# A low weight part made by a second ScalarE copy and an adding DMA, for one weight tile in eight

## The chip, the cores and the metric

The kernel runs on one core of one Trainium2 chip. The metric is the device time of one execution in microseconds. Five engines matter here: PE (TensorE, with its weight loads PEld), DVE (VectorE), ACT (ScalarE), POOL (GpSimd) and SP, whose queue issues the weight loads; 16 DMA engines move the data.

## What is computed

A decoder trunk of two layers on 256 tokens of 2048 features, all in fp32, each layer followed by an MLP with 8192 hidden units:

```
x += nsa_mixer(rmsnorm(x))        # three attention branches, one over compressed blocks
x += square(relu(rmsnorm(x) @ w_up[0])) @ w_down[0]
k, v = shared_kv(x)
x += diff_mixer(rmsnorm(x), k, v) # differential attention
x += square(relu(rmsnorm(x) @ w_up[1])) @ w_down[1]
out = rmsnorm(x)
```

Nearly all of the arithmetic is products of activations with weights. To keep fp32 accuracy each operand is cut into a high part, rounded to the type fp32r, and a low part, which is what the rounding left over; a product is then made of three matmuls (high by high, high by low, low by high).

## The kernel before

All weights pass through one stream, `plan`, of 368 units of 512 rows by 512 columns. A unit is two halves of 256 rows; a half is a tile of 128 partitions by 1024 elements (512 KB). `issue_raw` loads a half into a `raw` buffer by a DMA of SP's queue, `issue_split` makes from it the high part `wh` and the low part `wl`, and `unit_mm` or `up_unit` multiplies. `advance`, called as each unit is taken, issues loads up to four units ahead and splits up to two. Each of the tags `raw`, `wh` and `wl` has four buffers, so two units: a load waits until the split of the half two units earlier is done with `raw`, and a split waits until PE is done with the `wh` and `wl` of the half two units earlier.

The split is two instructions, line 146 on ACT and line 147 on DVE:

```
nc.scalar.activation(h, src, AF.Copy)
nc.vector.tensor_tensor(l, src, h.bitcast(F32), ALU.subtract)
```

The order of the work on PE and SP is that of the program; the other engines' queues are ordered by the scheduler, with the splits at high priority, and every queue is worked off in order. Attention heads, transposes and the norms are pieces that are put between the steps of the stream by a count of PE's time.

Stages of the stream by unit: 0 to 7 (first projections), 8 to 39 (projections, each followed by a unit of the compression product, which has only eight matmuls), 40 to 55 (queries, with heads between), 56 to 71 (output projection), 72 to 199 (first MLP: in each of four groups 16 up units, then 16 down units), 200 to 239 (keys, values, queries and output of the second layer), 240 to 367 (second MLP). In up units, `up_unit`, the weights are the stationary operand, and both halves are used until near the unit's end: the first half until three quarters of it. In the others the weights are the moving operand, and the first half is done in the middle of the unit.

Of the kernel before, what the change touches and what calls it, by code (L numbers as in the profile page):

```python
# [11 lines left out]
AF = mybir.ActivationFunctionType  # L12
ALU = mybir.AluOpType
AX = mybir.AxisListType

P = 128
# [4 lines left out]
EPS = 1e-6  # L21
NEG = -3.0e38
FLOOR = -1.0e38
# NSA heads: waits before the scores, the transposes and the values; head to head; first head
WAIT_A = (2.0, 12.5, 4.0, 1.5, 7.0)
# differential heads: the same, and before the normed output's transposes
WAIT_B = (1.0, 8.5, 5.0, 5.5, 9.0, 7.0)
LAMBDA_INIT = 0.8 - 0.6 * math.exp(-0.3 * 1)

# [2 lines left out]
def kernel(  # L32
# [22 lines left out]
    nc = tc.nc  # L55
# [14 lines left out]
    def T(shape, tag, dt=F32):  # L70
        return sb.tile(shape, dt, tag=tag, name=name(tag), bufs=BUFS[tag])
# [3 lines left out]
    def PT(tag):  # L75
        return pp.tile([P, 512], F32, tag=tag, name=name(tag), bufs=PB[tag])

# [1 line left out]
    # The weight products run as a steady stream; the pieces that wait on other  # L79
    # engines are generators, resumed between the stream's steps once the time  # L80
    # that they asked for has gone by on the tensor engine's own count.
    clock = [0.0]
    tasks = []
    seq = [0]
# [22 lines left out]
    def tick():  # L107
        if tasks and tasks[0][0] <= clock[0]:
            step()
# [21 lines left out]
    def mm(o, l, r, start, stop, shared=False):  # L131
        nc.tensor.matmul(o, lhsT=l, rhs=r, start=start, stop=stop, skip_group_check=shared)  # L132
        clock[0] += max(o.shape[-1], 256) / 2400.0

    def transpose(o, i, idn):
        nc.tensor.transpose(o, i, idn)  # L136
        clock[0] += 0.11
# [6 lines left out]
    def split(h, l, src, scale=None):  # L144
        if scale is None:
            nc.scalar.activation(h, src, AF.Copy)  # L146
            nc.vector.tensor_tensor(l, src, h.bitcast(F32), ALU.subtract)  # L147
        else:
            nc.scalar.activation(h, src, AF.Copy, scale=scale)
            nc.vector.scalar_tensor_tensor(l, src, scale, h.bitcast(F32), ALU.mult, ALU.subtract)  # L150

    ctx.enter_context(tc.manual_schedule(engines={mybir.EngineType.PE, mybir.EngineType.SP}))

# [1 line left out]
    cst = cp.tile([P, 640], F32, name="cst")  # L155
    ident = cst[:, 0:128]
    cmask = cst[:, 128:384]
# [20 lines left out]
    gates = cp.tile([P, 2, 48], F32, name="gates")  # L178
# [14 lines left out]
    def g_kv(k):  # L193
        return gcol2[:, 32 + k:33 + k]

# [1 line left out]
    plan = []  # L197

    def add_units(w, rows, c0):
# [12 lines left out]
        add_units(win, range(4), c * 512)  # L212

    def out_order():
        # (column chunk, head group): the later a group's heads come out, the later its part
        return ([(0, 0), (1, 0), (0, 1), (1, 1), (2, 0), (2, 1), (3, 0), (3, 1)] + [(2, 2), (3, 2), (0, 2), (1, 2)]
                + [(c, 3) for c in range(4)])

# [4 lines left out]
        add_units(nsa_w_out[0], [g], c * 512)  # L223

    def down_order(last):
        # (column chunk, quarter of the group's rows); at the very end the last quarters of two
        # chunks stay on chip and are used for one token tile after the other
        if not last:
            return [(c, u) for c in range(4) for u in range(4)]
        return ([(c, u) for c in range(2) for u in range(4)] + [(c, u) for c in (2, 3) for u in range(3)]  # L230
                + [(2, 3), (3, 3)])
# [17 lines left out]
    raws = {}  # L249
    units = {}  # L250
# [14 lines left out]
    def issue_split():  # L265
        i = pos["split"]
        if i >= len(plan):
            return
        pos["split"] += 1
        us = []  # L270
        for r in raws.pop(i):
            h = T([P, 2, 512], "wh", F32R)
            l = T([P, 2, 512], "wl", F32R)
            split(h, l, r)
            us.append((h, l))
        units[i] = us

# [20 lines left out]
                    start and kk == 0, stop and kk == 3)  # L298
                tick()

# [1 line left out]
    def new_stats():  # L302
        return T([P, 2, 4], "ss"), T([P, 2], "rs")

# [28 lines left out]
                          tp[:, kk * 256:(kk + 1) * 256], gf(k))  # L333

    def new_xt():
        # two tiles of eight feature blocks: [feature, block, part, token]
        return [T([P, 8, 2, S], "big", F32R) for _ in range(2)]

    def rope(dst, src, n, rot, ct, stb):
# [17 lines left out]
        return o  # L357

    def transpose_k(src, th, tl):
        # th, tl: [dk, kv head, token block, token]  # L360
        for pr in range(2):
            if pr:
                yield 0.8
            tp = PT("tp")
            for hh in range(2):
                for t in range(2):
                    h = pr * 2 + hh
                    transpose(tp[:, hh * 256 + t * P:hh * 256 + (t + 1) * P],
                              src[:, t, h * P:(h + 1) * P], ident)
            hs = slice(2 * pr, 2 * pr + 2)  # L370
            split(th[:, hs], tl[:, hs], tp.rearrange("p (h t q) -> p h t q", h=2, t=2))
# [5 lines left out]
    def new_kv(*shape):  # L377
        return T([P, *shape], "kv", F32R)


# [1 line left out]
    with tc.high_priority():  # L382
        for c in range(4):
            if c == 0:
# [16 lines left out]
        nc.vector.tensor_scalar(gsub, gcol2[:, 48:49], 1.0 - LAMBDA_INIT, None, ALU.mult)  # L401
        yield 0.0

    # =========================== layer 0: NSA ===========================
    ss, rs = new_stats()
    xt = new_xt()
    xts = [spawn(xt_chunk(c, [(lambda k: g_attn(0, k), xt)]), 5.5 * c - 2.0) for c in range(4)]
# [58 lines left out]
        X.append(T([P, 32, 120], "big", F32R))  # L466
        tX.append(spawn(make_X(tok, X[j], j)))

    # gates: the stationary operand holds both parts of the weights side by side
    gwp = [T([P, 8, 96], tag, F32R) for tag in ("wh", "wl")]  # L470
    for i in range(2):
        split(gwp[i][:, :, 0:48], gwp[i][:, :, 48:96], gw[:, 8 * i:8 * i + 8, :])
# [89 lines left out]
    half = cp.tile([P, 1], F32, name="half")  # L562
# [139 lines left out]
        return done  # L702

    def up_unit(us, ps, xt, k0):
        # weights stationary: the product comes out with the hidden units on partitions, the
        # part with the high half of the activations and the one with the low half side by side
        for pair in range(2):
            for kk in range(4):
                wh, wl = us[kk // 2]
                k = k0 + kk  # L710
                both = xt[k // 8][:, k % 8].rearrange("p s q -> p (s q)")
                for b in (2 * pair, 2 * pair + 1):
                    bs = slice(b * P, (b + 1) * P)
                    mm(ps[b], wh[:, kk % 2, bs], both, k == 0, False)
                    mm(ps[b][:, 0:S], wl[:, kk % 2, bs], both[:, 0:S], False, k == 15)
                tick()
# [75 lines left out]
    mlp(0, mxt, rs2, hook0, done)  # L792
    finish_stats(ssd, rsd)

    # =========================== layer 1: differential attention ===========================
    lamt = T([P, 256], "sbt")
    nc.gpsimd.dma_start(lamt, diff_lambda.rearrange("b f d -> b (f d)").to_broadcast([P, 256]))
    lv = lamt.rearrange("p (a b d) -> p a b d", a=2, b=2)
# [10 lines left out]
    ps = proj(kxt, before=xts)  # L809
    t_ = evac_tok(ps, rsd)  # L810
    rope(t_, t_, 8, 16, cosB, sinB)
    # keys of the two components side by side, each with zeros on the other's rows:
    # [.., kv head, (first tile: c0, c1; second tile: c0, c1), key]
    dkh, dkl, dv = new_kv(4, 4, P), new_kv(4, 4, P), new_kv(2, 4, 2, P)
    for d in (dkh, dkl):
        for cc in range(2):
            r = slice(64 - cc * 64, 128 - cc * 64)
# [18 lines left out]
    ready = [spawn(diff_keys(), 6.0)]  # L836
    ps = proj(kxt)
    for t in range(2):
        # [key, key tile, kv head, part, value column]
        split(dv[:, t, :, 0, :], dv[:, t, :, 1, :], ps[t].rearrange("p (g d) -> p g d", g=4), rsd[:, t:t + 1])  # L840

    oth, otl = T([P, 16, 256], "big", F32R), T([P, 16, 256], "big", F32R)
# [2 lines left out]
    def diff_head(hd, qr):  # L845
        g, i = hd // 4, hd % 4
# [44 lines left out]
        yield WAIT_B[2]  # L891
        yield from s_o.take()
        o = PT("tp")
        # columns: (first tile: main, low part of the values; second tile: the same)
        for t, blocks in ((0, ((0, 0),)), (1, ((1, 0), (2, 1)))):
            for n, (s_, kt) in enumerate(blocks):
                a = slice(s_ * P, (s_ + 1) * P)
# [68 lines left out]


def _consts():
    """Identity, causal masks and rotary tables: they depend on the shapes alone."""
    import numpy as np  # L970

    c = np.zeros((128, 640), np.float32)
    p = np.arange(128)
    c[:, 0:128] = np.eye(128, dtype=np.float32)
    c[:, 256:384] = np.where(p[None, :] <= p[:, None], 0.0, NEG)
    n = np.arange(32)
    for t in range(2):
        ok = (n[None, :] < 15) & (16 * n[None, :] + 31 <= (t * 128 + p)[:, None])
        c[:, 384 + 32 * t:416 + 32 * t] = np.where(ok, 0.0, NEG)

    def tables(head_dim, o):
        rot = head_dim // 4
        h = rot // 2
        e = (np.arange(0, rot, 2, dtype=np.float32) / np.float32(rot)).astype(np.float32)
        inv = (np.float32(1.0) / np.power(np.float32(500000.0), e)).astype(np.float32)
        ang = np.arange(S, dtype=np.float32)[:, None] * inv[None, :]
        cos, sin = np.cos(ang).astype(np.float32), np.sin(ang).astype(np.float32)
        for t in range(2):
            r = slice(t * 128, (t + 1) * 128)
            c[:, o + t * rot:o + t * rot + h] = cos[r]  # L990
            c[:, o + t * rot + h:o + (t + 1) * rot] = cos[r]
            b = o + 2 * rot + t * rot
            c[:, b:b + h] = -sin[r]
            c[:, b + h:b + rot] = sin[r]

    tables(128, 448)
    tables(64, 576)
    return c
# [24 lines left out]
```

## Time and profile before

| | |
|---|---|
| median of 3 runs | 2161.58 us (2161.39 to 2163.61) |
| profiled execution, span from the first to the last instruction | 2159.3 us |
| PE busy | 2135.1 us, 99% of the span |
| DVE busy | 1333.7 us, 62% |
| ACT busy | 1082.7 us, 50% |
| POOL busy | 81.4 us, 4% |
| read from HBM | 390.5 MB |

The span is that of one profiled execution, and the durations of its rows come from that one; the median is 2.3 us above it. Matmuls are pipelined: the record of one overlaps the next, so the step from one start to the next tells its pace.

### The profile page before, as it was taken

The numbers are of one execution on the slowest core, as the hardware profiler recorded it, in microseconds if no ns is written. First come the engines' busy times: TensorE is split into PE (matmuls) and PEld (weight loads), VectorE is DVE, ScalarE is ACT, GpSimd is POOL, SyncE is SP. The second block draws the span as 40 slices with busy tenths as digits, with TensorE's granted clock in tenths as the row PEclk, the third lists the DMA queues.
The fourth block names the chain that finished last, engine by engine and source line by source line (L and its number), as shares of the span: only waits on it lengthen the run. The fifth ranks groups of instructions, "written<-read, shape, count | busy, mean of one in ns | idle before, by whom it ended". The sixth has DMA issues, their size and how long they took to land.

```text
span 2159.3 us, 28803 instructions
## 1 busy us (share of the span) xinstructions
PE 2135.1 (99%) x10780; PEld 1794.7 (83%) x10780; DVE 1333.7 (62%) x2156; ACT 1082.7 (50%) x1737; POOL 81.4 (4%) x121
## 2 busy tenths in 40 slices
PE   8999999999999999999999999999999999999998
PEld 6877888888888888888888877888888888888886
DVE  5665777666546656555666578866656655655654
ACT  6665666454434434434555466664434434544443
POOL 0111100000000000000000111000000000000000
PEclk9999999999999999999999999999999999999999
DMA  7787432455566566666655543356566556566654
GB/s 244 238 266 242 124 100 90 145 171 184 196 194 189 193 194 186 195 195 188 188 191 185 185 146 127 127 186 188 193 194 186 195 194 187 187 199 190 192 193 142
DMA packets 204828, 394.45 MB, mean 183 GB/s; under 512 B 14176, under 2 KB 14368, under 8 KB 204560
## 3 DMA queue, kind: packets, MB, share of 16 engines
q1 hardware_dynamic: 203936, 390.51, 57.2%
q0 software_dynamic: 560, 2.02, 0.3%
q8 instruction: 84, 1.38, 0.3%
q14 instruction: 56, 0.46, 0.1%
q10 hardware_dynamic: 192, 0.08, 0.0%
HBM read 390.47 MB, written 2.10 MB: 182 GB/s over the span
## 4 chain that ended last, share of the span: by engine, by line
PE 94%; DVE 2%; ACT 1%; DMA 1%; issue 1%; POOL 0%; SPq 0%; DVEq 0%; POOLq 0%; ACTq 0%
PE acc L132 59%; PE tp L132 33%; PE tp L136 2%; DVE wl L147 1%; DMA raw<-in_nsa_w_in_dram 1%; ACT wh L146 1%; DMA raw<-in_nsa_cmp_w_dram 0%; ACT sa L874 0%; ACT sbt L874 0%; POOL sq L910 0%; DVE psl L147 0%; DVE big L150 0%; DVE sbt L881 0%; DVE pwl L906 0%; DVE pwl L912 0%
## 5 line engine op out<-in xcount | busy, mean ns | idle before, releaser
L147 DVE TENSOR_TENSOR wl<-raw,wh 128x1024 fp32r<-128x1024 f32 x736 | 902.4, 1228 | 711.9 <-ACT wh L146 705.4
L146 ACT ACTIVATE wh<-raw 128x1024 fp32r<-128x1024 f32 x736 | 777.8, 1058 | 825.4 <-PE acc L132 489.3
L132 PE MATMUL acc<-wh,big 128*128 128x512 f32 (+1 forms) x1600 | 548.0, 403 | 1.3 <-ACT wh L146 1.3
L132 PE MATMUL acc<-wh,kv 128*128 128x512 f32 x1280 | 397.2, 390 | 0.0
L132 PE MATMUL tp<-big,wh 128*128 128x512 f32 (+1 forms) x1040 | 359.5, 392 | 0.0
L132 PE MATMUL acc<-big,wh 128*128 128x512 f32 x1024 | 357.9, 394 | 0.0
L132 PEld LDWEIGHTS acc<-wh,big 128*128 128x128 f32 (+1 forms) x1600 | 300.9, 188 | 67.4 <-ACT wh L146 1.7
L132 PE MATMUL acc<-wl,big 128*128 128x512 f32 (+1 forms) x832 | 329.1, 396 | 0.5 <-DVE wl L147 0.5
L132 PE MATMUL tp<-big,wl 128*128 128x256 f32 (+1 forms) x1040 | 288.9, 280 | 0.0
L132 PE MATMUL acc<-big,wl 128*128 128x256 f32 x1024 | 286.8, 280 | 0.0
L132 PEld LDWEIGHTS acc<-wh,kv 128*128 128x128 f32 x1280 | 240.3, 188 | 50.1
L132 PE MATMUL acc<-wl,kv 128*128 128x512 f32 x640 | 249.0, 389 | 0.0
L132 PE MATMUL tp<-wh,kv 128*128 128x512 f32 x768 | 237.4, 389 | 0.0
L132 PEld LDWEIGHTS tp<-big,wh 128*128 128x128 f32 (+1 forms) x1040 | 194.3, 187 | 44.0
L132 PEld LDWEIGHTS acc<-big,wh 128*128 128x128 f32 x1024 | 192.3, 188 | 43.6
L132 PEld LDWEIGHTS tp<-big,wl 128*128 128x128 f32 (+1 forms) x1040 | 194.9, 188 | 0.0
L132 PEld LDWEIGHTS acc<-big,wl 128*128 128x128 f32 x1024 | 192.9, 188 | 0.2
L132 PEld LDWEIGHTS acc<-wl,big 128*128 128x128 f32 (+1 forms) x832 | 156.7, 188 | 31.3 <-DVE wl L147 1.0
L132 PEld LDWEIGHTS tp<-wh,kv 128*128 128x128 f32 x768 | 144.2, 188 | 29.9
L132 PE MATMUL tp<-wl,kv 128*128 128x512 f32 x384 | 149.4, 389 | 0.0
L132 PEld LDWEIGHTS acc<-wl,kv 128*128 128x128 f32 x640 | 120.2, 188 | 24.4
L146 ACT ACTIVATE kv<-q 128x256 fp32r<-128x256 f32 x128 | 50.0, 412 | 73.4 <-DVE q L735 73.4
(183 smaller groups left out, 1416.7 us busy)
## 6 DMA issues: line engine op xcount, KB each, us to landing
raw<-in_mlp_w_up_dram SPq DMA_DIRECT2D x256, 512.0 KB, 3.9
raw<-in_mlp_w_down_dram SPq DMA_DIRECT2D x256, 512.0 KB, 4.3
raw<-in_nsa_w_in_dram SPq DMA_DIRECT2D x80, 512.0 KB, 4.4
raw<-in_nsa_cmp_w_dram SPq DMA_DIRECT2D x32, 512.0 KB, 4.8
raw<-in_nsa_w_out_dram SPq DMA_DIRECT2D x32, 512.0 KB, 3.7
raw<-in_diff_w_q_dram SPq DMA_DIRECT2D x32, 512.0 KB, 3.7
raw<-in_diff_w_out_dram SPq DMA_DIRECT2D x32, 512.0 KB, 3.7
raw<-in_kv_w_shared_dram SPq DMA_DIRECT2D x16, 512.0 KB, 3.5
```

The costliest lines, as they stand in the source:

```text
L132: nc.tensor.matmul(o, lhsT=l, rhs=r, start=start, stop=stop, skip_group_check=shared)
L136: nc.tensor.transpose(o, i, idn)
L146: nc.scalar.activation(h, src, AF.Copy)
L147: nc.vector.tensor_tensor(l, src, h.bitcast(F32), ALU.subtract)
```

## The change

For the first half of every fourth unit (i % 4 = 2; 92 of 736 tiles) the low part is made in another way. ACT writes the high part `h` as before, then a second copy with the factor -1 into the buffer of the low part, which is minus the high part, and a DMA issued by POOL adds the weights to it in place. In every second of these tiles (i % 8 = 2) the DMA's source is the `raw` buffer on the chip, in the others it is the weights in HBM, read a second time. The other tiles stay as they were. The rest of the diff takes out comment lines.

```
-        for r in raws.pop(i):
+        for hf, r in enumerate(raws.pop(i)):
             h = T([P, 2, 512], "wh", F32R)
             l = T([P, 2, 512], "wl", F32R)
-            split(h, l, r)
+            if hf == 0 and i % 4 == 2:
+
+                nc.scalar.activation(h, r, AF.Copy)
+                nc.scalar.activation(l, r, AF.Copy, scale=-1.0)
+                src = r if i % 8 == 2 else plan[i][0:256].rearrange("(k p) c -> p k c", p=P)
+                nc.gpsimd.dma_start(l, src, accum_op=ALU.add)
+            else:
+                split(h, l, r)
             us.append((h, l))
         units[i] = us
```

## Rows read from the trace of the kernel before

**Rows 1.** The page's first line and the busy time of each engine.

```profile
span 2159.3 us, 28803 instructions
PE 2135.1 (99%) x10780; PEld 1794.7 (83%) x10780; DVE 1333.7 (62%) x2156; ACT 1082.7 (50%) x1737; POOL 81.4 (4%) x121
```

**Rows 2.** The chain that ended last, its shares of the span by engine.

```profile
by line: PE acc L132 59.3%; PE tp L132 32.6%; PE tp L136 2.2%; DVE wl L147 0.9%; DMA raw<-in_nsa_w_in_dram 0.8%; ACT wh L146 0.6%; issue 0.6%; DMA raw<-in_nsa_cmp_w_dram 0.2%; ACT sa L874 0.2%; ACT sbt L874 0.2%; POOL sq L910 0.2%; DVE psl 
```

**Rows 3.** Waits of PE: us in total, times, longest us.

```profile
PE tp L136 <- DMA cst<-in_consts_dram: 5.8, 1, 5.8
PE tp L136 <- DVE pwl L912: 1.9, 3, 1.2
...
PE acc L132 <- ACT wh L146: 1.3, 1, 1.3
...
PE tp L132 <- DVE qtl L147: 0.8, 2, 0.6
PE tp L132 <- DVE big L150: 0.7, 1, 0.7
PE tp L136 <- DVE pwl L906: 0.5, 1, 0.5
PE acc L132 <- DVE wl L147: 0.5, 1, 0.5
```

**Rows 4.** Timeline, compression stage, unit 22: start us, us, instruction [idle before <-releaser].

```profile
113.86 1.06 ACT L146 ACTIVATE wh<-raw 128x1024 fp32r<-128x1024 f32 x1 [1.45 <-PE acc L132]
...
118.55 0.40 PE L132 MATMUL acc<-wl,big 128*128 128x512 f32 x1
```

**Rows 5.** Timeline, first MLP, up products, unit 118.

```profile
706.88 1.05 ACT L146 ACTIVATE wh<-raw 128x1024 fp32r<-128x1024 f32 x1
...
707.96 2.50 DVE L147 TENSOR_TENSOR wl<-raw,wh 128x1024 fp32r<-128x1024 f32 x2 [0.53 <-ACT wh L146]
...
713.56 0.19 PEld L132 LDWEIGHTS tp<-big,wl 128*128 128x128 f32 x1
```

**Rows 6.** Timeline, first MLP, down products, unit 130.

```profile
771.12 1.06 ACT L146 ACTIVATE wh<-raw 128x1024 fp32r<-128x1024 f32 x1 [1.66 <-PE tp L132]
...
779.31 0.39 PE L132 MATMUL tp<-wl,kv 128*128 128x512 f32 x1
```

**Rows 7.** Timeline, values of the second layer, unit 206.

```profile
1192.49 1.06 ACT L146 ACTIVATE wh<-raw 128x1024 fp32r<-128x1024 f32 x1 [1.11 <-PE acc L132]
...
1201.79 0.39 PE L132 MATMUL acc<-wl,big 128*128 128x512 f32 x1
```

**Rows 8.** Groups of instructions: the two steps of a split.

```profile
L147 DVE TENSOR_TENSOR wl<-raw,wh 128x1024 fp32r<-128x1024 f32 x736 | 902.4, 1228 | 711.9 <-ACT wh L146 705.4
L146 ACT ACTIVATE wh<-raw 128x1024 fp32r<-128x1024 f32 x736 | 777.8, 1058 | 825.4 <-PE acc L132 489.3
```

**Rows 9.** DMA issues of POOL's queue: KB each, median us from issue to landing.

```profile
big<-in_final_norm_g_dram POOLq DMA_DIRECT2D x1, 1024.0 KB, 7.9
...
sbt<-in_diff_lambda_dram POOLq DMA_DIRECT2D x1, 128.0 KB, 3.4
```

**Rows 10.** SP's queue: packets, MB, share of 16 engines; then its up loads.

```profile
q1 hardware_dynamic: 203936, 390.51, 57.2%
...
raw<-in_mlp_w_up_dram SPq DMA_DIRECT2D x256, 512.0 KB, 3.9
```

**Rows 11.** Windows: length, busy us of each engine, PEclk, DMA share, GB/s.

```profile
68.00:195.00 127.00, 125.57 (x555) 100.15 (x554) 88.31 (x86) 78.14 (x85) 13.68 (x19) 1.00 0.85 269
...
625.00:1130.00 505.00, 505.00 (x2598) 431.63 (x2597) 294.02 (x361) 230.56 (x300) 0.00 (x0) 1.00 0.61 191
```

**Rows 12.** Waits of SP's queue: us in total, times, longest us.

```profile
SPq L261 <- DVE wl L147: 1413.6, 588, 10.2
```

**Rows 13.** The chain in order of time: one chunk of four up units.

```profile
702.62 22.19 PE tp L132 x128
```

**Rows 14.** Groups of POOL: the longest instruction of a rotary pass.

```profile
L351 POOL TENSOR_TENSOR q<-q,rb 128x256 f32<-128x256 f32 x11 | 12.0, 1090 | 0.9
```

## The prediction

> **What bounds the kernel now.** I read the page's head first: PE is busy for 2135.1 us of a span of 2159.3, DVE for 1333.7, ACT for 1082.7, POOL for 81.4 [rows 1]. The chain that ended last is PE in the weight products for nine tenths of its length, and DVE's `wl` has 1% of it [rows 2]. So the kernel is a stream of matmuls, with 24 us in which PE is idle. Then I asked what PE waited for: the longest wait is the load of constants at the start (5.8 us); a weight tile's high part cost it 1.3 us and a low part 0.5 us, once each in 736 tiles [rows 3]. Nothing that makes DVE faster can give back more than these crumbs. What counts is the reverse: by how much a low part may come later before PE stands still.
>
> **The room that each low part has.** With four `wh` and four `wl` buffers, the tile for unit i can be split only after PE has finished the tile two units earlier; ACT's idle time before `wh` is indeed put down to PE [rows 4, 6]. From that start I measured to the first PE instruction that reads the low part, for one unit of each kind that the edit touches (i with i % 4 = 2, first half). In the stage with the compression products (units 8 to 39, where short units of eight matmuls alternate with long ones): ACT starts at 113.86, the matmul is at 118.55, 4.69 us [rows 4]. In the up products: 706.88 to the weight load at 713.56, 6.68 us [rows 5]. In the down products: 771.12 to 779.31, 8.19 us [rows 6]. In the others, between which attention heads run, I show 1192.49 to 1201.79, 9.30 us [rows 7]. Now the low part is there early: in the up unit DVE begins at 707.96 and needs 1.25 us, so it ends 2.3 us after ACT's start, with 4.4 us to spare.
>
> **The change part by part.** There are 368 units, so 92 tiles are touched: 9 with the short room (8 in the compression stage and unit 2), 32 up, 32 down, 19 others.
>
> Removed: 92 subtractions at 1.23 us [rows 8], 113 us of DVE. They lie beside PE, so they are worth nothing, at most the 0.5 us that PE once waited for `wl` [rows 3].
>
> Added on ACT: 92 copies of the same shape as `wh<-raw`, 1.06 us each [rows 8], 97.5 us. ACT goes from 50% to 55% busy. The second half's copy queues behind the new one, so its low part (on DVE as before) comes up to 1.06 us later, inside a room of some 4 us; I take nothing. Without that cover it would be 92 x 1.06 = 98 us.
>
> Added on the path: the low part is now copy, copy, DMA issued by POOL, landing. The two copies and hand-overs take 2.2 us (2 x 1.06 plus an estimated 0.1), about what copy and subtraction take now. Then the whole landing time L of the adding DMA comes on top: a tile delays PE by 2.2 + L minus its room, where that is positive. PE takes its matmuls in order, so everything behind that one waits, and nothing later gives the time back.
>
> L is not in the trace, since no DMA of before adds. POOL's own DMAs bound it: 128 KB landed in 3.4 us, 1024 KB, among loads like the MLP's, in 7.9 us [rows 9]. The line through these two is 2.76 us + 5.02 ns per KB, so a plain 512 KB takes 5.3 us. An add must read two operands of 512 KB each; if each byte read counts, that is 1024 KB, 7.9 us. With the price of the SP queue's loads instead (57.2% of 2159.3 us for 745 loads of 512 KB is 1.66 us each [rows 10]) twice that on top of 2.76 us is 6.1 us, free of the loads that share the engines. Those are there: the DMA engines are 61% busy in the MLP stages and 85% in the compression stage [rows 11]. I take 7.0, midway between 6.1 and 7.9. The outer bounds are 3.4 us (the smallest transfer of POOL's queue) and 7.9 us.
>
> With L = 7.0 the chain is 9.2 us: 9 tiles x (9.2 - 4.69) = 40.6 us; 32 up x (9.2 - 6.68) = 80.6; 32 down x (9.2 - 8.19) = 32.3; the other 19 have room. The sum is 153.5 us. At 5.3 it is 25.3 + 26.2 = 51.5 us; at 7.9 it is 48.7 + 109.4 + 61.1 + 15.2 = 234 us; at 3.4 only 9 x 0.91 = 8 us.
>
> The skill has a price for L. The Trainium skill, DMA: Bandwidth & Descriptors (Anatomy of one DMA — SWDGE path), fits POOL's DMAs with 2.0 us plus bytes over 436 GB/s; for 1024 KB that is 4.4 us, and the sum would be 9 x (6.6 - 4.69) = 17 us. By that fit 128 KB would take 2.3 us, where the trace shows 3.4 [rows 9], so I hold to the rows. The Trainium skill, Collectives: The Full Stack (The bandwidth ceiling), finds an adding transfer 1.93 times as slow as a copy, because it reads two sources; by it L would be 2.76 + 1.93 x 2.57 = 7.7 us and the sum 216 us; no row here shows an add.
>
> Moved buffers: for the 46 tiles that add from `raw`, the buffer comes free when the DMA lands, not when DVE has read it. SP's queue waits for exactly that release already (1413.6 us in total [rows 12]), and it is in order, so the next loads start late too. In an up unit the load would start 9.2 us after the split, not 2.3, land 3.9 us later [rows 10], at 13.1, while its own split, two units of 5.55 us later (a chunk of four units takes 22.19 us [rows 13]), is due at 11.1 plus the stall of 2.5, so at 13.6. Just in time: nothing; if that cover is gone, the split's 4.4 us to spare comes next. The other 46 read their weights a second time, 24 MB on 390, and free `raw` a little earlier: nothing.
>
> POOL's queue: what stands behind a waiting DMA there are the rotary steps and the powers for the norms, 81.4 us in all [rows 1]; behind a rotary pass (six instructions, the longest of 1.1 us [rows 14]) the DMA can itself be late. POOL is busy for 13.7 us of the 127 of the compression stage [rows 11], so one of its nine tiles may meet such a pass: below 6.6 us, left out.
>
> **The rivals.** (a) The add costs little: L between 3.4 and 5.3, the read of the second operand hidden or the fixed part smaller, as by the fit above. Then only the compression stage and a sliver of the up products stall: 8 to 50 us, 2170 to 2212 us. For it: the SP queue lands 512 KB in 3.9 us [rows 10]. Against it: POOL's 128 KB needs 3.4.
> (b) It costs more: L above 7.9, or PE's clock falls after stalls. At L = 10 the sum is 67.6 + 176.6 + 128.3 + 55.1 = 428 us, 2589 us. The clock: all rows before are at 1.00 of 2.4 GHz [rows 11], and PE never idled over 1.3 us for a weight [rows 3], so nothing here shows what stalls of 2.5 to 4.5 us do. At the lower level, 1.2 GHz, one unit takes another 5.5 us; after the 9 longest stalls that is 50 us (2365), after all 41 above 2.5 us 226 us (2541).
> (c) The other side, not slower: the chain ends before PE comes. The place that decides is the compression stage: 2.2 + L must stay within 4.69, so L up to 2.5 us. Then the time is 2161.6 less at most the 0.5 us of [rows 3] (more only if DVE's 113 us free the few waits for its other results, 4.4 us in all with it [rows 3]). Against it: no POOL DMA of 128 KB or more lands under 3.4 us [rows 9].
>
> **How the numbers follow.** The profiled execution's span is 2159.3 us, the median of the runs 2161.58, 2.3 above it; I add to the median: 2161.6 + 153.5 = 2315 us. Chances: forecast (L 5.3 to 7.9, 2213 to 2396 us) 0.60; (a) 0.20; (b) 0.15; (c) 0.05, most of it no change. A measurement of this kernel tells about 0.2% (4.3 us) from no change. (a) and (b) are slower as well, so slower 0.95, same 0.04, faster 0.01. The range goes from the bound of L at 3.4, 2170, to L = 8.8 (56.8 + 138.2 + 89.9 + 32.3 = 317 us), 2480; it leaves out (c) and the greater part of (b).
>
> **What would show it.** Right: PE's waits in the changed profile name the low part's DMA in 70 to 90 tiles, longest in the compression stage (near 4.5 us), 2.5 us in up, 1 us in down products; issue to landing near 7 us; PE's busy time about the same and its idle time 24 + 150 us; up chunks of four units at 24.7 us for 22.19. Wrong: landings under 5 us (a), over 8 us or a granted clock under 1.00 inside the span (b), SP or ACT named as what PE waits for (then `raw` is late and the cover above was none), or no new wait (c).

## The result and the profile after

The changed kernel takes 2342.5 us (median of 4 runs, 2341.8 to 2346.6) for 2161.5 before; the ratio is 1.084, with a 95% interval from 1.0827 to 1.0854. The prediction was 2315 us, range 2170 to 2480. The profiled execution has a span of 2344.8 us for 2159.3, 185.5 us more.

The page's head after; it answers to [rows 1].

```profile
span 2344.8 us, 29065 instructions
PE 2204.6 (94%) x10780; PEld 1832.4 (78%) x10780; DVE 1219.9 (52%) x2064; ACT 1165.6 (50%) x1829; POOL 170.9 (7%) x213
```

PE has the same 10780 matmuls. Its busy time is 69.5 us longer, and its idle time went from 24.2 to 140.2 us, 116.0 more; 69.5 + 116.0 is the whole difference. So there are two losses, one in waiting and one in matmuls that themselves take longer.

What PE waited for, after (us in total, times, longest us); it answers to [rows 3].

```profile
PE tp L132 <- DMA wl<-in_mlp_w_up_dram: 52.7, 16, 4.6
PE acc L132 <- DMA wl<-in_nsa_w_in_dram: 23.5, 4, 6.3
PE acc L132 <- DMA wl<-in_mlp_w_down_dram: 18.9, 10, 2.7
PE acc L132 <- DMA wl<-raw: 12.4, 7, 2.4
PE tp L132 <- DMA wl<-in_mlp_w_down_dram: 7.5, 6, 2.6
...
PE acc L132 <- DMA wl<-in_kv_w_shared_dram: 0.6, 1, 0.6
```

These six lines sum to 115.6 of the 116.0 us: the added waiting is the adding DMA. They are also lopsided. The 46 adds from HBM cost 103 us, the 46 from `raw` 12. The DMA issues show why (KB each, median us from issue to landing; they answer to [rows 9]):

```profile
wl<-raw POOLq DMA_DIRECT2D x46, 512.0 KB, 5.0
...
wl<-in_mlp_w_up_dram POOLq DMA_DIRECT2D x16, 512.0 KB, 8.2
wl<-in_mlp_w_down_dram POOLq DMA_DIRECT2D x16, 512.0 KB, 9.2
...
wl<-in_nsa_w_in_dram POOLq DMA_DIRECT2D x7, 512.0 KB, 9.2
```

Two neighbouring up tiles in the timeline, first one that adds from `raw` (unit 114), then one that adds from HBM (unit 118); start us, us, instruction. The second is the tile of [rows 5].

```profile
755.48 1.06 ACT L276 ACTIVATE wh<-raw 128x1024 fp32r<-128x1024 f32 x1
756.45 1.04 ACT L277 ACTIVATE wl<-raw 128x1024 fp32r<-128x1024 f32 x1
757.78 0.91 POOL L279 DMA_DIRECT2D wl<-raw  x1 [27.89 <-ACT wl L277]
759.72 3.41 SPq L261 DMA_DIRECT2D raw<-in_mlp_w_up_dram  x2
762.78 0.19 PEld L132 LDWEIGHTS acc<-big,wl 128*128 128x128 f32 x1 [0.29 <-DMA wl<-raw]
...
778.32 1.06 ACT L276 ACTIVATE wh<-raw 128x1024 fp32r<-128x1024 f32 x1
779.29 1.04 ACT L277 ACTIVATE wl<-raw 128x1024 fp32r<-128x1024 f32 x1
780.35 7.75 SPq L261 DMA_DIRECT2D raw<-in_mlp_w_down_dram  x4
780.62 1.20 POOL L279 DMA_DIRECT2D wl<-in_mlp_w_up_dram  x1 [21.93 <-ACT wl L277]
788.08 0.19 PEld L132 LDWEIGHTS tp<-big,wl 128*128 128x128 f32 x1 [2.75 <-DMA wl<-in_mlp_w_up_dram]
```

Both have copy, copy, issue, and both issue 2.3 us after ACT's start. With `raw` as the source, SP's next load comes 1.9 us after the issue, and PE waits 0.3 us. With HBM as the source, ACT's second copy was the last reader of `raw`, so SP starts its loads at 780.35, 0.27 us before POOL's add, and the low part comes 7.5 us after its issue.

The other loss is the clock: the granted clock is the share of 2.4 GHz at which PE was let run. Four stretches around a down tile's wait, after (length, busy us of PE, PEld, DVE, ACT, POOL, granted clock, DMA share, GB/s):

```profile
829.00:832.00 3.00, 3.00 (x15) 2.40 (x13) 1.23 (x1) 1.06 (x1) 0.00 (x0) 1.00 1.04 213
832.00:835.00 3.00, 0.29 (x2) 0.00 (x0) 1.22 (x1) 1.06 (x1) 0.00 (x0) 1.00 1.04 345
835.00:838.00 3.00, 2.98 (x7) 2.41 (x8) 0.00 (x0) 0.00 (x0) 0.00 (x0) 0.53 0.62 229
839.00:842.00 3.00, 3.00 (x15) 2.45 (x14) 1.22 (x1) 1.06 (x1) 0.00 (x0) 1.00 0.00 0
```

PE works, stands still for 2.7 us, and comes back at a granted clock of 0.53, that is nearly all at 1.2 GHz: 7 matmuls start in 3 us, not 15. Over the span the mean granted clock is 0.974, so (1 - 0.974) x 2344.8 = 61 us of full-speed time are missing (before, at 0.999, it was 2 us), most of the 69.5 us. Not each wait has this after it: from 785.4 to 788.1 PE stands still for 2.4 us (unit 118), from 1123.6 to 1127.0 for 3.4 us, longer than the wait above, and the stretches behind them are at 1.00:

```profile
785.40:788.10 2.70, 0.28 (x3) 0.03 (x1) 2.12 (x2) 1.04 (x1) 0.00 (x0) 1.00 1.00 302
788.10:792.00 3.90, 3.90 (x22) 3.44 (x23) 0.00 (x0) 0.00 (x0) 0.00 (x0) 1.00 0.65 236
...
1123.60:1127.00 3.40, 0.00 (x0) 0.00 (x0) 1.86 (x2) 0.79 (x1) 0.00 (x0) 1.00 1.01 310
1127.10:1131.10 4.00, 4.00 (x23) 3.50 (x24) 0.00 (x0) 0.00 (x0) 0.00 (x0) 1.00 0.44 156
```

### The profile page after: what moved, and what is told of

It reads as the page before. It is cut to its first block, busy times and chain, and to the rows that moved or that the text cites. A ratio compares the mean times of both kernels' runs of the same rounds, so it can differ in the third digit from the quotient of the medians.

```text
span 2344.8 us, 29065 instructions
## 1 busy us (share of the span) xinstructions
PE 2204.6 (94%) x10780; PEld 1832.4 (78%) x10780; DVE 1219.9 (52%) x2064; ACT 1165.6 (50%) x1829; POOL 170.9 (7%) x213
## 3 DMA queue, kind: packets, MB, share of 16 engines
q0 software_dynamic: 19696, 50.26, 11.8%
## 4 chain that ended last, share of the span: by engine, by line
PE 73%; DMA 15%; ACT 3%; DVE 2%; issue 1%; POOL 0%; POOLq 0%; DVEq 0%; ACTq 0%; SPq 0%
PE acc L132 46%; PE tp L132 25%; DMA wl<-in_mlp_w_down_dram 6%; DMA wl<-in_mlp_w_up_dram 6%; ACT wl L277 2%; PE tp L136 2%; DMA wl<-raw 2%; DMA wl<-in_nsa_w_in_dram 1%; DVE wl L147 1%; ACT wh L146 0%; DMA wl<-in_kv_w_shared_dram 0%; DMA raw<-in_nsa_w_in_dram 0%; ACT sbt L881 0%; ACT sa L881 0%; ACT wh L276 0%
## 5 line engine op out<-in xcount | busy, mean ns | idle before, releaser
L147 DVE TENSOR_TENSOR wl<-raw,wh 128x1024 fp32r<-128x1024 f32 x644 | 787.5, 1226 | 959.4 <-ACT wh L146 952.5
L146 ACT ACTIVATE wh<-raw 128x1024 fp32r<-128x1024 f32 x644 | 678.8, 1057 | 854.8 <-PE acc L132 461.0
L132 PE MATMUL acc<-wh,big 128*128 128x512 f32 (+1 forms) x1600 | 556.3, 409 | 1.0 <-ACT wh L146 1.0
L132 PE MATMUL acc<-wh,kv 128*128 128x512 f32 x1280 | 403.9, 396 | 0.0
L132 PE MATMUL tp<-big,wh 128*128 128x512 f32 (+1 forms) x1040 | 383.9, 411 | 0.0
L132 PE MATMUL acc<-wl,big 128*128 128x512 f32 (+1 forms) x832 | 335.5, 403 | 34.4 <-DMA wl<-in_nsa_w_in_dram 23.5
L132 PE MATMUL tp<-big,wl 128*128 128x256 f32 (+1 forms) x1040 | 302.3, 293 | 52.7 <-DMA wl<-in_mlp_w_up_dram 52.7
L132 PEld LDWEIGHTS tp<-big,wl 128*128 128x128 f32 (+1 forms) x1040 | 206.3, 199 | 57.8 <-DMA wl<-in_mlp_w_up_dram 57.8
L132 PEld LDWEIGHTS tp<-big,wh 128*128 128x128 f32 (+1 forms) x1040 | 205.7, 198 | 49.1
L132 PEld LDWEIGHTS acc<-wl,kv 128*128 128x128 f32 x640 | 122.4, 191 | 48.3 <-DMA wl<-in_mlp_w_down_dram 23.1
L277 ACT ACTIVATE wl<-raw 128x1024 fp32r<-128x1024 f32 x92 | 96.9, 1053 | 55.2 <-PE acc L132 36.8
```

The lines of the kernel that those rows point to most:

```text
L277: nc.scalar.activation(l, r, AF.Copy, scale=-1.0)
```

## The experiments

Theory: an adding DMA is late where the chain of copy, issue and landing is longer than the room of the tile's buffer; from HBM it is later because the same choice of source lets SP's loads out beside it; the lower clock comes on top of the longer waits. Rivals: one landing time for all, whatever the source; HBM reads that are slow by themselves; ACT's added copies; the added traffic. A time without an interval is that of one run; the kernel before took 2161.3 to 2163.2 us on the chips of these runs.

**All from raw, and all from HBM.** The edit of the first:

```
-                src = r if i % 8 == 2 else plan[i][0:256].rearrange("(k p) c -> p k c", p=P)
+                src = r
```

> All 92 adds read the raw buffer on the chip, none reads HBM. Theory A (what counts is the source of the add: the profile of the changed kernel lands the adds from raw in 5.0 us and those from HBM in 8 to 9 us): landing stays near 5 us for all, PE waits about 2.3 us in each of 9 tiles of the first stages and under 0.6 us in the 32 up tiles, nothing in down; some 2190 to 2200 us, granted clock above 0.99. Rival B (one L for all of about 7 us, as the prediction had it): 2300 to 2345 us.

Measured: 2210.2 us, 49 above the kernel before; landing 4.9 us; PE waits 23.1 us, all in nine tiles; mean clock 0.993. Theory A holds for the source, though the time is 10 us over its figure.

The second takes the HBM expression in all 92 tiles.

> All 92 adds read the weights from HBM a second time. Theory A: every tile behaves as the 46 from HBM do now, so the 103 us of waits on those double to some 206 us and the work lost to the lower clock (69 us of PE busy time more than before) nearly doubles too: 2450 to 2500 us, landing 8 to 9 us. Rival B (the source does not matter): unchanged, about 2340 us.

Measured: 2462.6 us; landings 8.0 to 9.1 us; the waits for the adds sum to 204 us (twice 103 is 206); mean clock 0.964. So twice the tiles from HBM give twice the waits.

**The loads held back.** In the 46 tiles from HBM a POOL instruction of one column reads `raw` and the finished low part, so that SP's next load has to wait for the landing:

```
                 nc.gpsimd.dma_start(l, src, accum_op=ALU.add)
+                if i % 8 != 2:
+                    nc.gpsimd.tensor_tensor(hold, r[:, 0, 0:1], l[:, 0, 0:1].bitcast(F32), ALU.add)
```

> After each add from HBM a one-column POOL instruction reads both the raw buffer and the finished low part, so that the next load into this raw buffer can't start before the add has landed, as it already is with the adds from raw. Theory E (the adds from HBM land late because the loads that SP then issues get into the DMA engines first): landing from HBM falls from 8 to 9 us to some 6 us and the time to 2220 to 2270 us. Rival F (reading HBM for an add is slow by itself): landing stays at 8 us or more and the time at 2340 us or above, since the loads are later.

Measured: 2246.4 us, 96 us less, with the same bytes from the same sources. The landings and PE's waits of this run:

```profile
wl<-in_mlp_w_up_dram POOLq DMA_DIRECT2D x16, 512.0 KB, 6.3
wl<-in_mlp_w_down_dram POOLq DMA_DIRECT2D x16, 512.0 KB, 7.5
wl<-in_nsa_w_in_dram POOLq DMA_DIRECT2D x7, 512.0 KB, 6.0
```

```profile
PE tp L132 <- DMA wl<-in_mlp_w_up_dram: 23.8, 16, 1.8
PE acc L132 <- DMA wl<-raw: 13.4, 6, 2.4
PE acc L132 <- DMA wl<-in_nsa_w_in_dram: 13.2, 4, 3.9
PE acc L132 <- DMA wl<-in_mlp_w_down_dram: 3.6, 5, 1.1
```

The wait in up tiles fell from 52.7 to 23.8 us and in down tiles from 26.4 to 5.5, and the mean clock is 0.993. Theory E holds in that the loads that are let out make the add late; rival F falls as the main cause, though 6.0 to 7.5 us are not yet the 4.9 of the adds from `raw`.

**One piece for two.** The adds from HBM read 128 rows of 1024 columns (`wide` holds these slices) in place of 256 rows of 512:

```
-                src = r if i % 8 == 2 else plan[i][0:256].rearrange("(k p) c -> p k c", p=P)
+                src = r if i % 8 == 2 else wide[i].rearrange("p (k c) -> p k c", k=2)
```

> The adds from HBM read 128 rows of 1024 columns of the same matrix (4 KB in one piece for each partition) in place of 256 rows of 512 (two pieces of 2 KB), so the low parts of these 46 tiles get other numbers; bytes, sources and order stay. Theory G (the number of pieces makes the adds from HBM late: POOL's issue takes 1.2 us for them and 0.9 us for those from raw): issue 0.9 us, landing 6 to 7 us, time 2250 to 2290 us. Rival (the loads that are let through set it): landing stays at 8 us and more, time 2325 us or above.

Measured: 2280.4 us. POOL's issues of this run (ns min/median/max, first and last start) against 1.20 us for the HBM ones after:

```profile
L281 POOL DMA_DIRECT2D wl<-raw x46: 853/864/953, 23.2 to 2229.5; - x46
L281 POOL DMA_DIRECT2D wl<-in_mlp_w_up_dram x16: 853/862/866, 531.8 to 2162.1; - x16
```

Issue falls by 0.34 us, landing to 7.3 us in up and 7.5 in down tiles, the up waits from 52.7 to 37.5 us. Theory G has its time, but the landings stay above the 6 to 7 us that it named. The form of the read (larger pieces, and half as many) and SP's loads both make the add late; which share each has when both are changed was not tried.

**Copy without adding.** The `accum_op` is left out.

> The 92 DMAs copy the weights into the low part's buffer without adding, so the low part is the weight itself and the products are other numbers. Theory C (the add reads two operands, so the movement takes twice that of a copy, 3.1 for 1.6 us): landings fall by about 1.5 us, to 3.5 us from raw and 7 us from HBM, and the time to 2230 to 2260 us. Rival D (the adding costs nothing, the fixed part and what is in the engines' queues cost it all): landings and time as with the add, about 2340 us.

Measured: 2217.0 us; landings 3.5 us from `raw`, 5.1 (up) and 7.1 us (down) from HBM. The engines' time for POOL's queue is 7.1% of a span of 2215.2 us, in the run with the add 11.8% of 2344.8; less the 6.5 us that the queue already took before (0.3% of 2159.3), that is 1.64 and 2.94 us for each DMA. The add takes 1.8 times a copy. Theory C holds for the price of the add, and 125 of the 181 us go with it; the up landings fell by 3.1 us, more than its 1.5, and the time is 13 us under its figure.

**The second copy alone.** The DMA goes, and DVE makes the low part again:

```
-                nc.gpsimd.dma_start(l, src, accum_op=ALU.add)
+                nc.vector.tensor_tensor(l, r, h.bitcast(F32), ALU.subtract)
```

> The second ScalarE copy stays in the 92 tiles, but the low part is then made by VectorE as in the kernel before (its subtraction overwrites the copy); no adding DMA. If the copy lies beside PE, as the prediction has it: the time of before, 2161 to 2165 us. Rival (ACT's queue is part of the loss: each copy delays the second half's high part or an attention head): up to 92 x 1.06 = 98 us more, 2180 to 2260 us.

Measured: 2167.3 us, ratio 1.0023, interval 1.0014 to 1.0033, about 5 us. The rival's 20 to 98 us did not come, but the copies are not quite free.

**Negative copy first.** The copy with -1 and the DMA stand ahead of the high part's copy.

> The negative copy and the DMA stand ahead of the high part's copy in all 92 tiles. In the profile of the changed kernel the scheduler has that order already in the down units and most others, while in the up units the high part goes first. Theory (the chain ahead of the add counts in full): each of the 16 up tiles from HBM gets its low part 0.95 us earlier, 15 us, the 16 from raw lose their stalls of some 0.3 us, and a few stretches at the lower clock go: 2310 to 2328 us. Rival (the landing alone sets it, or the loads of SP move along): unchanged at 2340 us.

Measured: 2316.8 us, within the figure. The up waits fell from 52.7 to 40.4 us, 12.3 us where 15 were expected. The landings in up tiles stayed at 8.2 us, though SP's next loads now come after the add's issue has begun. In the down units little changed (24.1 us of waits for 26.4), since there the scheduler had put the negative copy first already, as this part of the timeline of the changed kernel shows (unit 134):

```profile
871.88 1.06 ACT L277 ACTIVATE wl<-raw 128x1024 fp32r<-128x1024 f32 x1 [1.43 <-PE tp L132]
872.84 1.04 ACT L276 ACTIVATE wh<-raw 128x1024 fp32r<-128x1024 f32 x1
...
873.23 1.20 POOL L279 DMA_DIRECT2D wl<-in_mlp_w_down_dram  x1 [20.86 <-ACT wl L277]
...
873.91 9.06 SPq L261 DMA_DIRECT2D raw<-in_mlp_w_up_dram  x4
```

Here `raw` comes free only with the high part's copy, and SP's loads go out 0.7 us after the add's issue has begun. The add lands late all the same (the median is 9.2 us in down tiles), so a load need not be issued first to delay the add.

**An own buffer.** On top of that, the low part of the 92 tiles gets its own tag, with one buffer (`wx=1`), so it need not wait for PE to leave a `wl` buffer; the rotary scratch moves to another tag to make room.

```
-            l = T([P, 2, 512], "wl", F32R)
+            l = T([P, 2, 512], "wx" if hf == 0 and i % 4 == 2 else "wl", F32R)
...
-        b = T([P, 2, n, rot], "rb")
+        b = T([P, 2, n, rot], "sbt")
```

> As the run with the negative copy first, but the low part of the 92 tiles gets a buffer tag of its own (to make room for it the rotary scratch shares another tag), so that copy and add no longer wait for PE to leave a low part's buffer and can start some 3 us earlier. Same sources, same number of bytes. Theory (the whole loss is lateness at PE, the traffic itself costs nothing): nearly all of it goes, up and down stages back at the pace of before, a few us of waits left in the compression stage: 2161 to 2185 us, granted clock at 0.99 or more. Rival (the 50 MB more of adding traffic slow the weight loads or the matmuls): 2220 us or more even so.

Measured: 2207.3 us, ratio 1.0208, interval 1.0191 to 1.0225. That is 22 us over the theory's figure. The stages separate it (columns as in the windows above):

```profile
70.00:210.00 140.00, 117.81 (x478) 92.20 (x477) 66.79 (x67) 72.78 (x81) 16.82 (x23) 0.91 0.75 229
...
660.00:1160.00 500.00, 500.00 (x2573) 427.87 (x2572) 263.05 (x331) 246.31 (x312) 22.99 (x22) 1.00 0.71 215
```

The same windows of the changed kernel:

```profile
70.00:210.00 140.00, 114.49 (x467) 89.26 (x467) 64.63 (x67) 69.42 (x78) 17.75 (x24) 0.91 0.74 225
660.00:1160.00 500.00, 472.71 (x2343) 398.10 (x2342) 234.44 (x289) 218.01 (x269) 21.26 (x21) 0.98 0.66 196
```

In the first MLP PE has no idle time at all and the full clock, although the adds still take 7.3 us in up and 8.2 us in down tiles from issue to landing and the DMA engines are 71% busy. The compression stage is nearly as bad as with the shared buffer: 22 us idle in 140 for 26, clock 0.91 in both.

**An own buffer, all from raw.**

> As the run with its own buffer, and all 92 adds read raw. The raw buffer is then held until the add has landed in every tile. Theory: landing near 5 us and started early, so no low part is late, not even in the compression stage: 2161 to 2166 us, no faster than the kernel before, since PE's matmuls are the bound and VectorE's 113 us were beside them. Rival (VectorE's work taken away is worth something): below 2157 us. Rival (held raw buffers make SP's loads late): 2175 us or more, with PE or ACT waiting for loads.

Measured: 2198.6 us, ratio 1.0166, interval 1.015 to 1.0181. The figure was missed, and so was the landing near 5 us. All of PE's waits for adds, 20.3 us in 8 tiles, are in the first stages. The landings of this run, and one of the waits in the timeline:

```profile
wx<-raw POOLq DMA_DIRECT2D x92, 512.0 KB, 6.8
```

```profile
122.63 1.06 ACT L276 ACTIVATE wx<-raw 128x1024 fp32r<-128x1024 f32 x1 [0.18 <-DMA raw<-in_nsa_w_in_dram]
122.98 1.50 SPq L261 DMA_DIRECT2D raw<-in_nsa_cmp_w_dram  x2
123.99 0.85 POOL L278 DMA_DIRECT2D wx<-raw  x1 [16.43 <-ACT wx L276]
132.75 0.19 PEld L132 LDWEIGHTS acc<-wx,big 128*128 128x128 f32 x1 [4.20 <-DMA wx<-raw]
...
132.76 0.51 PE L132 MATMUL acc<-wx,big 128*128 128x512 f32 x1 [3.77 <-DMA wx<-raw]
```

Here the copy waits for its weights, which have only just come, so an own buffer gains little; SP issues two loads, the first of them a microsecond earlier than the add, and this add from `raw` takes 8.8 us too. The same adds from `raw` landed in 4.9 us with the shared buffer and in 6.8 us with an own one, which starts them earlier: the source does not decide alone, what else is under way does too.

**The control, and an own buffer from unit 40 on.** The control is the kernel before with the rotary scratch moved.

> The kernel before, with nothing changed but the rotary scratch sharing the tag of the heads' score tiles, as the two runs with an own buffer needed it. It is the control for them: in their profiles PE also stood still in the stages with attention heads. If that came from this sharing: 2170 to 2185 us. If it came from the adds: 2161 to 2165 us.

Measured: 2162.7 us, ratio 0.9998, interval 0.9989 to 1.0008: the move costs nothing, so the move of the rotary scratch is not what makes the runs with an own buffer slower.

The other has the own buffer for `i >= 40` alone:

> As the run with an own buffer and both sources, but only from unit 40 on (82 tiles); the 10 tiles before keep the split of the kernel before. If all of the loss outside the first stages was lateness of the low parts, this takes the time of the control with the shared scratch, within 0.3%, with PE waiting for no adding DMA. Rival (the traffic or ACT's copies cost something by themselves): 10 us or more above the control.

Measured: 2170.3 us, ratio 1.0034, interval 1.002 to 1.0047; no adding DMA is among PE's waits, and both MLPs run without idle time at the full clock. Over the control it is 7.6 us, 0.35%, between the theory's 0.3% and the rival's 10 us. The profiled executions show where most of it is: PE's idle time is 28.5 us for the control's 24.5, its busy time 2139.9 for 2135.7, and the granted clock falls in the second layer's stage with attention heads (this run, then the control):

```profile
1150.00:1480.00 330.00, 322.38 (x1552) 261.74 (x1551) 218.09 (x527) 203.41 (x439) 46.41 (x65) 0.98 0.58 176
1150.00:1480.00 330.00, 323.97 (x1584) 263.55 (x1583) 235.67 (x542) 195.45 (x430) 35.27 (x53) 1.00 0.50 160
```

The second copy alone had cost 5 us, so most of the 7.6 may be ACT's copies among the heads; POOL's queue, which now holds the adds as well as the rotary steps, was not tried apart from them. No version tried is faster than the kernel before: with DVE relieved of 82 subtractions and no wait for an add, the time is still above.

## Why the prediction was right, point by point

**Right: the direction and the mechanism.** PE in order, a fixed room for each tile, the landing longer than the room, and DVE's 113 us worth nothing (the versions with the waits gone are not faster). The sum of 153.5 us stands against 181 us measured (185.5 in the profiled execution), but it was not reached by its own terms, and that it is so near is in part luck. Of the prediction's own signs of being right, waits in 70 to 90 tiles and a PE busy time that stays the same did not come: the waits are in 44 tiles, and the busy time is 69.5 us longer. Two signs that it had set for rival (b), landings over 8 us and a granted clock under 1.00, did come.

**Mis-sized: the landing time L.** One value of 7.0 us was taken; it is 5.0 us from `raw` and 7.7 to 9.2 us from HBM (8.2 in up, 9.2 in down tiles). The middle is close to 7, but the waits are not: the tiles from HBM cost 103 us and those from `raw` 12, in all 115.6 for 153.5. By stage, the up tiles took 52.7 us from HBM and some 2.6 of the 12.4 from `raw` (forecast 80.6), the down tiles 26.4 (32.3), the first stages the remaining 33 (40.6).

**Failed: "The other 46 read their weights a second time ... and free `raw` a little earlier: nothing."** That was where the money went. Freed early, `raw` lets SP's loads out beside the add, just ahead of its issue in the up units and during it in the down units: holding them back gave 96 us. For the 46 that hold `raw` the text expected no harm from the late loads, and there was none; it missed that the hold keeps the add's way clear.

**Failed: "the low part is now copy, copy, DMA" in every tile.** It is so in the up units. In the down units and in most others ACT's negative copy runs first, and the issue comes 1.35 us after ACT's start rather than 2.3. By the prediction's own rule, with the order of the up units the landings of 9.2 us would cost about 16 x (2.3 + 9.2 - 8.19) = 53 us there, with this order 16 x (1.35 + 9.2 - 8.19) = 38. The measured 26.4 us is below both; the other 11 us are not explained.

**Mis-sized: the clock.** It was a rival, priced at 50 to 226 us and at nothing in the sum; it costs about 61 us of full-speed time, a third of the loss. The forecast came within 27 us of the measured time because waits 38 us too high and a clock term left out cancel in part; that is luck.

**Nearly right: ACT's copies at nothing.** They cost 5 us by the run with the second copy alone.

**The price from a page.** The run without the add bears out the doubling that the prediction took for its upper bound: 2.94 against 1.64 us of the engines' time, 1.8 times. The Trainium skill, Collectives: The Full Stack (The bandwidth ceiling), measures an all-gather, which copies, 1.93 times as fast as a reduce-scatter, whose add reads two sources; the 1.8 here is near it. By the fit in the Trainium skill, DMA: Bandwidth & Descriptors (Anatomy of one DMA — SWDGE (gpsimd) path), a plain 512 KB would take an estimated 3.2 us; the copies from `raw` landed in 3.5, those from HBM, in competition with loads, in 5.1 to 7.3.

**Left open.** Why the loads delay an add as long as they do was not taken apart; neither was the clock's part separated by a run that has the waits without the lower clock. Which waits are followed by 1.2 GHz is not settled: one of 2.7 us with it, and one of 3.4 us without, are shown above.

## What to carry to other kernels

Before work is moved from a compute engine to a DMA, measure the room from the buffer's release to the first reader, and set the whole landing time against it, not the DMA's share of bandwidth. Ask also what the moved step releases: a source that is read early frees its buffer early, and the transfer which that lets out may hold up the one that is urgent. On a kernel bound by PE, a wait costs its length and may cost more in the clock after it: here 116 us of waits went with some 60 us of lost clock.

## What the runs showed of the hardware that was not expected

- An adding DMA of POOL's queue took 2.94 us of the 16 engines per 512 KB, a copy 1.64.
- The same add landed in 4.9 us from `raw` and 8.0 to 9.1 us from HBM with loads let out beside it; with the loads held back 5.9 to 7.5 us from HBM. From `raw`, started earlier into a buffer of its own, it took 6.8 us.
- POOL's issue of an add took 0.86 us with one piece of 4 KB for each partition in HBM and 1.20 us with two pieces of 2 KB.
- After a wait of 2.7 us PE's granted clock was 0.53 over the next 3 us; after another of 3.4 us it stayed at 1.00.
